# Squares and head sums moved to VectorE, and other banks for the indexer, in a two-layer decoder trunk

## The chip, the cores and the metric

The kernel runs on one core of a Trainium2 chip. The metric is the device time of one execution in microseconds, from runs of the whole program; the profile shows one further execution. The engines are TensorE (PE in the profile; its weight loads are PEld), VectorE (DVE), ScalarE (ACT), GpSimd (POOL) and SyncE (SP), which here only issues DMAs.

## The reference

A trunk of two layers over 512 tokens of width 1024, batch 1, float32. Layer 0 is a half-step SwiGLU, a mixer of Mamba-2 SSD heads and mLSTM heads, and a second half-step SwiGLU. Layer 1 is the same with sparse attention as its mixer. Before each of the six stages the tokens are normalized by their root mean square:

```
x = x + 0.5 * swiglu(rms_norm(x, ffn_norm[l, 0]), ...)
h = rms_norm(x, mix_norm[l]);  x = x + mixer(h)
x = x + 0.5 * swiglu(rms_norm(x, ffn_norm[l, 1]), ...)
rms_norm(x, g) = x * rsqrt(mean(x * x) + 1e-6) * g
```

The sparse attention (16 heads of 64, one shared key and value head) lets each query see only the 128 keys that an indexer scores highest. The indexer has 8 heads; its score is a weighted sum over them, with weights `wi` that depend on the query:

```
logits = einsum('bthd,bsd->btsh', qi, ki)
score  = einsum('btsh,bth->bts', relu(logits), wi) * idx_scale      # then causal mask
sel    = top_k(score, 128);  softmax attention over the selected keys
```

## The kernel before

All activations stay on the chip, transposed: `xT` holds the 1024 features in 8 chunks of 128 partitions, with the 512 tokens along the free dimension. Weights are streamed as float32 blocks through a ring of 4 raw buffers, and each is split into a high and a low part (ScalarE copies the high part, VectorE or an accumulating DMA makes the low one). A product is then three matmuls: high by high, high by low and low by high (`mm3`, lines 241 to 243).

**The order of the work.** Every operation is not issued at once but given to a `Plan` as a step, with an engine, an estimated duration, and the keys of what it reads and writes. At the end one list scheduler places the steps of the whole program: on each engine it takes the step that can start first by its estimates, and among those the one that is due first. TensorE's steps are kept in order within a stream; the attention stage has several streams ("filler", "index", "logits", "values"), and filler products have their due times pushed back (`plan.later`), so that they stand in gaps. Tiles with few buffers (`plan.BUFS`, PSUM banks among them) make a step wait for the users of the tile that had the buffer before. Each engine then runs its instructions in the order so written.

**The norm between stages.** When the stage before has finished a pair of chunks, `prep_later` (from line 634) makes, per chunk, the input times its gain in a high and a low part (L657 on ScalarE, L660 on VectorE) and its square (L669 on ScalarE). GpSimd adds the squares chunk by chunk to a running sum `ssq` (L356, called with `pool` true). The squares of the last two chunks are not added: they are appended to the list `ssqs`. `settle_later` (from line 615) is called twice by the next stage. The first call sums over the partitions on TensorE: for each member of `ssqs` and each of the four token blocks, a matmul with a column of ones (L327, tile `pssq`). VectorE then makes the mean (L624) and GpSimd the power of -1/2 (L626). The second call spreads the factors over the partitions with four transposes (L336, tile `prow`) and a copy on ScalarE (L630), which gives `rrow`. The products themselves start before `rrow` is known; they are scaled afterwards. In an FFN's first units (`unit`, from line 576) each of eight steps is a block of four products of 0.69 us by the planner, and the two calls stand behind the second and the fourth block (behind the third and the fifth where `late` is set, in the first FFN). The mixer of layer 0 calls `settle_later` at places of its own.

**The indexer in attention.** Seven jobs (`indexer`) project the tokens to the indexer's queries, keys and weights; a job is a product over 8 chunks into one PSUM bank, and `scaled` copies it out on ScalarE with the norm's factors (L1595). The first four jobs use banks `gm`, `po` and two of `lg`, and run before the factors are known; the last three use `gm`, `po` and `gm` again. Then, for each query block b = 1, 2, 3 with n = 256, 384 or 512 keys: rotary embedding on VectorE (L1507 to L1511), transposes (L1521), and four pairs of logits (L1665), one pair for two heads, into `lg` banks. ScalarE applies the relu into `rl` (L1672). GpSimd has made 8 diagonal matrices from the head weights (L1648); TensorE multiplies each `rl` by its diagonal and accumulates the 8 in one bank (`acc`, tag `pt`, L1656); ScalarE copies the sum into the mask's place (L1676); GpSimd sets the causal part (L1677). `topk` then runs 16 rounds on VectorE, each of a maximum of eight (L1883) and a replacement (L1884), and turns the scores into a mask (L1887). Meanwhile the filler stream makes the key and value projection and the attention's queries, and the softmax of the heads (L1784 logits, L1788 mask and maximum, L1800 exponentials, L1806, L1824 values) follows block by block, block 0 needing no top-k.

Of the kernel before, what the change touches and what calls it, by code (L numbers as in the profile page):

```python
# [16 lines left out]
P = 128  # L17
# [196 lines left out]
class Trunk:  # L214
# [361 lines left out]
    def unit(self, raws, stream, late, summed):  # L576
# [6 lines left out]
        for qs in ((0, 1), (2, 3)):  # L583
            for i in range(4):
# [6 lines left out]
                for s in range(2):  # L591
                    col = slice(s * P, (s + 1) * P)
                    for q in qs:
# [5 lines left out]
                        )  # L599
                if 2 * qs[0] + i in ((2, 4) if late else (1, 3)):  # L600
                    self.settle_later()
# [32 lines left out]
    def prep_later(self, which, k, last, squares=True, half=None):  # L634
# [18 lines left out]
        for j in (k, k + 1):  # L653
# [15 lines left out]
            self.s(n, lambda x=x, sq=sq: nc.scalar.activation(sq()[:, cols], x, AF.Square), self.xk(j, halves), sk)  # L669
            if last:  # L670
                self.ssqs, self.ssqk = self.ssqs + [(sq, halves[0] * NB // 2)], self.ssqk + sk
            elif j:
                part = [lambda x=x: x()[:, cols] for x in (ssq, sq)]
                self.vtt(n, part[0], *part, ALU.add, ["ssq"], ["ssq"] + sk, True)
        if last:
# [861 lines left out]
    def attention(self, nxt):  # L1537
# [23 lines left out]
        keep, kept = self.spot("keep", (4 * T,), 1)  # L1561
        diags, diagk = self.spot("diag", (2, 8, P), 1)
        two = [self.spot("pr", (2, 2 * T), 2) for _ in range(2)]
# [41 lines left out]
        scaled(jobs)  # L1605
        for b, g, tag in ((2, 1, "gm"), (3, 0, "po"), (3, 1, "gm")):
            jobs = [(b, g, self.bank(tag))]
            indexer(jobs, (0, 1, 2, 3, 6, 7, 4, 5))
            scaled(jobs)
# [17 lines left out]
        for b in range(NB):  # L1627
# [15 lines left out]

            acc, acck = self.bank("pt")
            diag = []
            for h in range(8):
                d, dk = lambda h=h, b=b: diags()[:, b % 2, h], (*diagk, b % 2, h)
                self.plan.add("gpsimd", 0.4, lambda d=d, t=t, h=h: nc.gpsimd.tensor_scalar(  # L1648
                    d(), self.ident, t()[:, WI + h : WI + h + 1], 0.0, op0=ALU.mult, op1=ALU.add), [xk], [dk])
                diag.append((d, dk))  # L1650
            rls = []

            def add(acc=acc, acck=acck, diag=diag, rls=rls, n=n):
                for h in range(len(rls) - 2, len(rls)):
                    (d, dk), (rl, rk) = diag[h], rls[h]
                    self.t(0.02 + 1.68e-3 * n, lambda h=h, d=d, rl=rl: nc.tensor.matmul(  # L1656
                        acc()[:, 0:n], d(), rl()[:, 0:n], start=h == 0, stop=h == 7), [dk, rk], [acck])

            for i in range(4):
                ps = [self.bank("lg") for _ in range(2)]  # L1660

                def pair(ps=ps, qiT=qiT, i=i, n=n):
                    for par in range(2):
                        hp = slice(par * 64, par * 64 + 64)
                        nc.tensor.matmul(ps[par][0]()[:, 0:n], qiT()[hp, i * P : (i + 1) * P], kiT()[hp, 0:n], start=True, stop=True)  # L1665

                self.t(0.1 + 1.68e-3 * n, pair, [qik] + [(*kik, s) for s in range(b + 1)], [ps[0][1], ps[1][1]])
                if i:
                    add()
                for par in range(2):  # L1670
                    rl, rk = self.spot("rl", (T,), 4)
                    self.s(n, lambda rl=rl, ps=ps, par=par, n=n: act(rl()[:, 0:n], ps[par][0]()[:, 0:n], AF.Relu, scale=IDX_SCALE),  # L1672
                           [ps[par][1]], [rk])
                    rls.append((rl, rk))
            add()
            self.s(n, lambda sc=sc, acc=acc, n=n: act(sc(), acc()[:, 0:n], AF.Copy), [acck], [sk])  # L1676
            self.p(64, lambda sc=sc, b=b, n=n: nc.gpsimd.affine_select(  # L1677
# [285 lines left out]
```

## Time and profile before

| | |
|---|---|
| runs, median of 3 | 2012.17 us (2010.16 to 2013.01) |
| profiled execution, own time | 2003.96 us |
| its span, first to last instruction | 2002.2 us |
| mean granted TensorE clock | 0.992 |
| TensorE busy, loads busy | 98%, 91% of the span |
| VectorE, ScalarE, GpSimd busy | 81%, 63%, 16% |

In a profile row of the page or of a grouping, the line of the kernel comes first (L327), then engine and operation, the tile written and the tiles read, the shapes, and the count; then busy time, the mean duration of one, and the idle time of the engine just before, with what ended it. A row of the timeline begins with start and duration in us; brackets at its end show idle time of that engine before it and what ended that. A row of a stretch shows its bounds and length, and then the busy time of PE, PEld, DVE, ACT and POOL with the instruction counts, the granted TensorE clock (1.00 is full speed), the DMA engines' busy share and GB/s. A matmul of two float32 operands that were not split counts as two instructions.

### The profile page before, as it was taken

The numbers are of one execution on the slowest core, as the hardware profiler recorded it, in microseconds if no ns is written. First come the engines' busy times: TensorE is split into PE (matmuls) and PEld (weight loads), VectorE is DVE, ScalarE is ACT, GpSimd is POOL, SyncE is SP. The second block draws the span as 40 slices with busy tenths as digits, with TensorE's granted clock in tenths as the row PEclk, the third lists the DMA queues.
The fourth block names the chain that finished last, engine by engine and source line by source line (L and its number), as shares of the span: only waits on it lengthen the run. The fifth ranks groups of instructions, "written<-read, shape, count | busy, mean of one in ns | idle before, by whom it ended". The sixth has DMA issues, their size and how long they took to land.

```text
span 2002.2 us, 36425 instructions
## 1 busy us (share of the span) xinstructions
PE 1956.5 (98%) x14674; PEld 1813.3 (91%) x14674; DVE 1627.8 (81%) x2373; ACT 1264.7 (63%) x1906; POOL 325.0 (16%) x401
## 2 busy tenths in 40 slices
PE   8999999999999999999999999999999999999998
PEld 6999999799888888999998999999866588999998
DVE  6888888887888558989788998878589647988886
ACT  6666656567777545766566566666747744757564
POOL 1000002222234110000012001001414521101010
PEclk9999999999999999999999999999899999999999
DMA  8566766467769342666654466565735202666564
GB/s 221 137 157 152 176 155 161 118 166 190 198 176 262 86 117 74 162 172 162 158 149 141 111 170 161 155 174 137 188 88 116 53 17 69 158 158 169 148 170 115
DMA packets 226609, 292.89 MB, mean 146 GB/s; under 512 B 15036, under 2 KB 196488, under 8 KB 225928
## 3 DMA queue, kind: packets, MB, share of 16 engines
q1 hardware_dynamic: 200728, 199.30, 32.2%
q0 software_dynamic: 25632, 91.24, 24.2%
q8 instruction: 115, 1.88, 0.4%
q14 instruction: 54, 0.44, 0.1%
q10 hardware_dynamic: 80, 0.02, 0.0%
HBM read 192.96 MB, written 6.33 MB: 100 GB/s over the span
## 4 chain that ended last, share of the span: by engine, by line
PE 76%; DVE 8%; DMA 8%; issue 5%; ACT 1%; POOL 1%; SPq 0%; POOLq 0%; ACTq 0%; DVEq 0%
PE pA L242 9%; PE pA L241 9%; PE pA L243 9%; PE pD L241 5%; PE pD L243 5%; PE pD L242 5%; DMA form<-raw 3%; PE hm L242 2%; PE hm L243 2%; PE hm L241 2%; PE pB L241 2%; PE pB L243 2%; PE pB L242 2%; DMA raw<-in_hy_w_in 2%; DVE raw L356 2%
## 5 line engine op out<-in xcount | busy, mean ns | idle before, releaser
L363 DVE TENSOR_TENSOR form<-raw,form 128x1024 fp32r<-128x1024 f32 (+2 forms) x382 | 454.9, 1195 | 101.5 <-ACT form L361 100.0
L361 ACT ACTIVATE form<-raw 128x1024 fp32r<-128x1024 f32 (+2 forms) x382 | 392.1, 1030 | 206.0 <-DVE raw L356 142.4
L392 POOL DMA_DIRECT2D form<-raw x172 | 150.9, 879 | 1344.3 <-ACT form L391 1298.3
L356 DVE TENSOR_TENSOR raw<-raw 128x1024 f32<-128x1024 f32 (+2 forms) x281 | 333.2, 1190 | 22.8 <-DMA raw<-in_ffn_w_down 9.0
L241 PE MATMUL pA<-xf,form 128*128 128x256 f32 x1152 | 321.2, 279 | 0.0
L243 PE MATMUL pA<-xf,form 128*128 128x256 f32 x1152 | 320.7, 278 | 0.0
L242 PE MATMUL pA<-xf,form 128*128 128x256 f32 x1152 | 320.7, 278 | 0.0
L391 ACT ACTIVATE form<-raw 128x1024 fp32r<-128x1024 f32 (+1 forms) x172 | 178.2, 1037 | 161.6 <-PE pD L243 74.4
L241 PEld LDWEIGHTS pA<-xf,form 128*128 128x128 f32 x1152 | 217.2, 188 | 0.3
L243 PEld LDWEIGHTS pA<-xf,form 128*128 128x128 f32 x1152 | 217.3, 189 | 0.0
L242 PEld LDWEIGHTS pA<-xf,form 128*128 128x128 f32 x1152 | 217.0, 188 | 0.2
L242 PE MATMUL pA<-hid,form 128*128 128x256 f32 x704 | 198.2, 282 | 3.3 <-DVE hid L363 3.3
L241 PE MATMUL pA<-hid,form 128*128 128x256 f32 x704 | 198.0, 281 | 0.6 <-ACT hid L361 0.5
L243 PE MATMUL pA<-hid,form 128*128 128x256 f32 x704 | 197.2, 280 | 0.0
L393 ACT ACTIVATE form<-raw 128x1024 fp32r<-128x1024 f32 (+1 forms) x172 | 176.5, 1027 | 0.0
L241 PE MATMUL pD<-xf,form 128*128 128x256 f32 x576 | 160.3, 278 | 0.0
L243 PE MATMUL pD<-xf,form 128*128 128x256 f32 x576 | 160.2, 278 | 0.0
L242 PE MATMUL pD<-xf,form 128*128 128x256 f32 x576 | 160.2, 278 | 0.0
L356 DVE TENSOR_TENSOR ft<-ft 128x256 f32<-128x256 f32 (+2 forms) x296 | 151.3, 543 | 3.6
L242 PEld LDWEIGHTS pA<-hid,form 128*128 128x128 f32 x704 | 132.4, 188 | 5.2 <-DVE hid L363 5.1
L241 PEld LDWEIGHTS pA<-hid,form 128*128 128x128 f32 x704 | 132.6, 188 | 1.4 <-ACT hid L361 0.7
L508 ACT ACTIVATE ft<-pA 128x512 f32<-128x512 f32 x120 | 71.5, 595 | 97.7 <-PE pA L243 90.0
(441 smaller groups left out, 5427.6 us busy)
## 6 DMA issues: line engine op xcount, KB each, us to landing
form<-raw POOLq DMA_DIRECT2D x156, 512.0 KB, 5.9
raw<-in_ffn_w_gate SPq DMA_DIRECT2D x88, 512.0 KB, 3.9
raw<-in_ffn_w_up SPq DMA_DIRECT2D x88, 512.0 KB, 4.1
raw<-in_ffn_w_down SPq DMA_DIRECT2D x64, 512.0 KB, 4.0
raw<-in_hy_w_in SPq DMA_DIRECT2D x44, 512.0 KB, 4.7
raw<-in_ffn_w_down SPq DMA_DIRECT2D x32, 384.0 KB, 3.1
raw<-in_hy_w_out SPq DMA_DIRECT2D x16, 512.0 KB, 4.2
form<-raw POOLq DMA_DIRECT2D x16, 384.0 KB, 4.2
```

Source lines behind the costliest of these rows:

```text
L241: mm(out, l[0], r[0], start=start, stop=False)
L242: mm(out, l[0], r[1], start=False, stop=False)
L243: mm(out, l[1], r[0], start=False, stop=stop)
L356: (self.p if pool else self.v)(n, lambda: e.tensor_tensor(out(), x(), y(), op=op), reads, writes)
L361: self.s(n, lambda: nc.scalar.activation(hi(), src(), AF.Copy), srck, hik)
L363: n, lambda: nc.vector.tensor_tensor(lo(), src(), hi().bitcast(F32), op=ALU.subtract), srck + hik, lok
L391: self.s(n, lambda: nc.scalar.activation(f()[:, 1], raw, AF.Copy, scale=-1.0), rawk, lok)
L392: self.plan.add("gpsimd", 0.85, lambda: nc.gpsimd.dma_start(f()[:, 1], raw, accum_op=ALU.add), rawk + lok, lok, 5.5)
L393: self.s(n, lambda: nc.scalar.activation(f()[:, 0], raw, AF.Copy), rawk, hik)
L508: self.s(T, lambda: nc.scalar.activation(to(), ps()[:, :, 0:H], AF.Copy), [(*psk, 0), (*psk, 1)], tok)
```

## The change

Four edits.

In `unit`, the two calls of `settle_later` stand behind the third and the fourth block, where they stood behind the second and the fourth (the `late` case stays).

In `prep_later`, the squares of the last two chunks are added to the running sum too, by VectorE (`vtt` with `pool` false), so that `ssqs` has one member. This holds for all five norms between stages.

In `attention`, the last three jobs of the indexer use the banks `pt`, `pt` and the third `lg`.

In `attention`, the diagonals, their products, the bank `acc` and the copy out of it are gone. For each head VectorE multiplies `rl` by the head's weight, a column of the projection, and adds it to the scores in place (`scalar_tensor_tensor`; a `tensor_scalar` for the first head).

```
-                if 2 * qs[0] + i in ((2, 4) if late else (1, 3)):
+                if 2 * qs[0] + i in ((2, 4) if late else (2, 3)):
                     self.settle_later()
...
-            if last:
-                self.ssqs, self.ssqk = self.ssqs + [(sq, halves[0] * NB // 2)], self.ssqk + sk
-            elif j:
+            if j:
                 part = [lambda x=x: x()[:, cols] for x in (ssq, sq)]
-                self.vtt(n, part[0], *part, ALU.add, ["ssq"], ["ssq"] + sk, True)
+                self.vtt(n, part[0], *part, ALU.add, ["ssq"], ["ssq"] + sk, not last)
...
-        diags, diagk = self.spot("diag", (2, 8, P), 1)
...
-        for b, g, tag in ((2, 1, "gm"), (3, 0, "po"), (3, 1, "gm")):
+        for b, g, tag in ((2, 1, "pt"), (3, 0, "pt"), (3, 1, "lg")):
             jobs = [(b, g, self.bank(tag))]
             indexer(jobs, (0, 1, 2, 3, 6, 7, 4, 5))
             scaled(jobs)
...
-            acc, acck = self.bank("pt")
-            diag = []
-            for h in range(8):
-                d, dk = lambda h=h, b=b: diags()[:, b % 2, h], (*diagk, b % 2, h)
-                self.plan.add("gpsimd", 0.4, lambda d=d, t=t, h=h: nc.gpsimd.tensor_scalar(
-                    d(), self.ident, t()[:, WI + h : WI + h + 1], 0.0, op0=ALU.mult, op1=ALU.add), [xk], [dk])
-                diag.append((d, dk))
-            rls = []
-
-            def add(acc=acc, acck=acck, diag=diag, rls=rls, n=n):
-                for h in range(len(rls) - 2, len(rls)):
-                    (d, dk), (rl, rk) = diag[h], rls[h]
-                    self.t(0.02 + 1.68e-3 * n, lambda h=h, d=d, rl=rl: nc.tensor.matmul(
-                        acc()[:, 0:n], d(), rl()[:, 0:n], start=h == 0, stop=h == 7), [dk, rk], [acck])
...
-                if i:
-                    add()
                 for par in range(2):
                     rl, rk = self.spot("rl", (T,), 4)
+                    h = 2 * i + par
+                    wi = lambda t=t, h=h: t()[:, WI + h : WI + h + 1]
                     self.s(n, lambda rl=rl, ps=ps, par=par, n=n: act(rl()[:, 0:n], ps[par][0]()[:, 0:n], AF.Relu, scale=IDX_SCALE),
                            [ps[par][1]], [rk])
-                    rls.append((rl, rk))
-            add()
-            self.s(n, lambda sc=sc, acc=acc, n=n: act(sc(), acc()[:, 0:n], AF.Copy), [acck], [sk])
+                    if h:
+                        self.v(n + 60, lambda rl=rl, sc=sc, wi=wi, n=n: v.scalar_tensor_tensor(
+                            sc(), rl()[:, 0:n], wi(), sc(), op0=ALU.mult, op1=ALU.add), [rk, xk, sk], [sk])
+                    else:
+                        self.v(n, lambda rl=rl, sc=sc, wi=wi, n=n: v.tensor_scalar(
+                            sc(), rl()[:, 0:n], wi(), 0.0, op0=ALU.mult, op1=ALU.add), [rk, xk], [sk])
```

## The prediction

> **What bounds the kernel now.** I read the page's busy shares and its chain of waits first, then busy time by stretches, then the timeline at the places that the change touches.
>
> ```profile
> span 2002.2 us, 36425 instructions
> PE 1956.5 (98%) x14674; PEld 1813.3 (91%) x14674; DVE 1627.8 (81%) x2373; ACT 1264.7 (63%) x1906; POOL 325.0 (16%) x401
> PE 76%; DVE 8%; DMA 8%; issue 5%; ACT 1%; POOL 1%; SPq 0%; POOLq 0%; ACTq 0%; DVEq 0%
> ...
> 1447.00:1454.00 7.00, 7.00 (x40) 5.26 (x37) 0.00 (x0) 4.37 (x10) 2.23 (x5) 1.00 1.01 187
> 1454.00:1577.00 123.00, 117.09 (x541) 72.62 (x539) 104.90 (x320) 79.72 (x182) 45.06 (x68) 0.99 0.38 84
> ...
> 1538.00:1577.00 39.00, 33.09 (x176) 17.97 (x174) 29.15 (x94) 34.21 (x87) 22.81 (x36) 0.96 0.20 41
> ```
>
> TensorE is the bound: 98% busy, and 76% of the chain that ended last is its work. So a TensorE instruction that goes away is worth its own time, unless TensorE then waits for something else. The last three rows (columns: stretch, length, then busy us of PE, PE loads, DVE, ACT, POOL, the granted clock, DMA) are the attention stage, from the indexer's first block to the first logits of the last block. TensorE idles 123.00 - 117.09 = 5.9 us there, all of it after 1538 (39.00 - 33.09), when the products that fill its gaps have run out. VectorE, at 104.90 of 123 us, is the nearest second bound.
>
> **1. The sums of squares.** Five times, at each norm between stages, 24 one-column matmuls (12 in two passes) sum the squares over features: 8 for the running sum and 8 for each of the two last squares that were left apart. The change adds those two on VectorE, so 8 of 24 stay.
>
> ```profile
> 359.12 2.73 PE L327 MATMUL pssq<-raw,ssq 128*128 128x1 f32 x24
> ...
> 1429.89 2.73 PE L327 MATMUL pssq<-raw,ssq 128*128 128x1 f32 x24
> ...
> 1661.16 3.55 PE L327 MATMUL pssq<-raw,ssq 128*128 128x1 f32 x24 [0.88 <-POOL ssq L356]
> ```
>
> 2.73 us for 24 is 0.114 us each; 16 fewer are 1.82 us, and five places give **9.1 us**. TensorE is busy on both sides in all five, so I take it whole.
>
> At the norm before the last FFN TensorE also waited 0.88 us for the running sum. The change puts the sums one block of products later in a unit, which covers this wait: **0.9 us**, and what is late next is the second step, the row of factors. Both steps now have one block between them instead of two. The two rows below bound a block: its first product starts at 1669.84 and the transposes of the factors follow at 1672.62, 2.8 us. From the sums' end to the factors I count from the two rows after: VectorE's step 0.1 us behind the last matmul (1085.14 + 2.74), then GpSimd's power until 1088.15 + 1.47 = 1089.62, together 1.8 us. It fits with 1 us to spare; if VectorE has one 1.2 us split ahead of its step, the stall is 0.2 us. I take nothing.
>
> ```profile
> 1669.84 0.43 PE L241 MATMUL pu<-xgn,form 128*128 128x512 f32 x1
> ...
> 1672.62 0.60 PE L336 MATMUL prow<-raw 128*128 128x128 f32 x4
> ...
> 1085.14 2.74 PE L327 MATMUL pssq<-raw,ssq 128*128 128x1 f32 x24
> ...
> 1087.91 0.16 DVE L624 TENSOR_SCALAR raw<-pssq 128x4 f32<-128x4 f32 x1
> 1088.15 1.47 POOL L626 TENSOR_TENSOR raw<-raw 128x4 f32<-128x4 f32 x1 [5.58 <-DVE raw L624]
> ...
> 352.54 0.41 PE L242 MATMUL hc<-xgn,form 128*24 128x512 f32 x1 [1.30 <-DVE xgn L660]
> ...
> 1081.49 0.50 PE L242 MATMUL pg<-xgn,form 128*128 128x512 f32 x1 [1.01 <-DVE xgn L660]
> ```
>
> The price is on VectorE: two adds of 128x512 at 0.69 us (the L718 row below) in each of five places, 6.9 us in all. Behind them on VectorE stand conversions of the normalized input (L660) and splits of weights. Where VectorE is idle they cost nothing; in the two rows above TensorE already waits 1.30 and 1.01 us for L660. Bounds: 0, and all 6.9 us on the path. The adds need the last squares, and so come after most of the conversions that TensorE waits for; I charge **1.0 us**.
>
> **2. The clock.** Four stretches below hold or follow these sums.
>
> ```profile
> 360.00:370.00 10.00, 10.00 (x48) 8.37 (x48) 2.75 (x5) 1.08 (x2) 1.04 (x1) 0.83 0.34 99
> 750.00:760.00 10.00, 10.00 (x60) 8.69 (x59) 6.05 (x21) 0.88 (x2) 1.53 (x3) 1.00 0.18 54
> 1085.00:1095.00 10.00, 10.00 (x60) 8.70 (x59) 5.30 (x8) 1.74 (x3) 1.47 (x1) 1.00 0.51 160
> 1430.00:1440.00 10.00, 8.96 (x55) 8.52 (x54) 3.38 (x10) 3.83 (x11) 5.45 (x9) 0.72 1.03 261
> 1440.00:1450.00 10.00, 10.00 (x63) 8.33 (x62) 2.14 (x4) 7.90 (x15) 6.87 (x12) 0.94 0.42 105
> 1660.00:1670.00 10.00, 9.12 (x40) 7.76 (x39) 2.91 (x5) 2.50 (x5) 2.12 (x2) 0.66 0.12 42
> ```
>
> After three of the five bursts the granted clock falls (0.83; 0.72 with 0.94; 0.66): 1.7, 2.8 + 0.6 = 3.4 and 3.4 us of full-speed time lost, 8.5 us in all. After the other two it stays at 1.00, so the same 2.73 us burst does it only sometimes, as if activity were judged over fixed stretches not much longer than the burst. A burst of 8, 0.9 us, should be too short. Bounds: 0 (other causes keep them) and 8.5 us. I take the two dear ones, **6.8 us**, and leave 1.7 us for a new stretch where TensorE will wait more, in attention.
>
> The Trainium skill ("TensorE: Matmul & The Clock Gate", section "Why this matters for your kernels") says that the clock falls back after an idle gap of about 3 us. Here TensorE was busy through the bursts at 359 and idle for under 1 us around 1430 and 1661, so the trace does not follow that rule as written; by it the burst would not matter and this term would be 0.
>
> **3. The weighted sum over heads.** It removes 48 matmuls (24 in two passes), 24 diagonals on GpSimd and 3 copies on ScalarE.
>
> ```profile
> L1648 POOL TENSOR_SCALAR diag<-raw,pr 128x128 f32<-128x128 f32 x24 | 13.9, 634 | 2.1 <-ACT pr L1595 2.1
> ...
> L1656 PE MATMUL pt<-rl,diag 128*128 128x512 f32 x16 | 7.7, 605 | 0.0
> ...
> L1656 PE MATMUL pt<-rl,diag 128*128 128x384 f32 x16 | 6.0, 506 | 0.0
> ...
> L1656 PE MATMUL pt<-rl,diag 128*128 128x256 f32 x16 | 4.3, 398 | 0.0
> ...
> 1481.10 3.60 PE L1656 MATMUL pt<-rl,diag 128*128 128x512 f32 x8
> 1484.13 0.79 PE L241 MATMUL gm<-form,xgn 128*128 128x512 f32 x1
> ```
>
> Busy time is 7.7 + 6.0 + 4.3 = 18.0 us with overlapping tails. By starts, the eight of 512 columns took 1484.13 - 1481.10 = 3.03, 0.379 each; scaled by columns 16 x 0.379 x (512 + 384 + 256) / 512 = 13.6 us. I take 15 us of TensorE. GpSimd's 13.9 us cover nothing: it is 16% busy.
>
> What it adds is VectorE work, priced from these rows (128x512 scalar_tensor_tensor; 128x256 of two tensors; a 384-wide form at its least 0.547; tensor_scalar of 256, 384 and 512):
>
> ```profile
> L718 DVE SCALAR_TENSOR_TENSOR raw<-ft,raw x72: 677/691/1758, 116.6 to 1994.4; 128x512 f32<-128x512 f32 x72
> L356 DVE TENSOR_TENSOR raw<-lg,raw x16: 411/424/425, 1630.4 to 1660.3; 128x256 f32<-128x256 f32 x16
> L1788 DVE CUSTOM_DVE_ANT_0 pw<-lg,keep x32: 547/610/692, 1548.7 to 1605.6; 128x384 f32<-128x384 f32 x16, 128x512 f32<-128x512 f32 x16
> L1887 DVE TENSOR_SCALAR keep<-keep x3: 329/355/424, 1472.2 to 1554.1; 128x256 f32<-128x256 f32 x1, 128x384 f32<-128x384 f32 x1, 128x512 f32<-128x512 f32 x1
> 1454.28 0.43 DVE L1883 MAX8 keep<-keep 128x8 f32<-128x256 f32 x1 [12.11 <-POOL keep L1677]
> ```
>
> Block 1: 7 x 0.42 + 0.36 = 3.3 us, covered by the 12.11 us in which VectorE waits for that block's scores. Block 2: 7 x 0.55 + 0.33 = 4.2; block 3: 7 x 0.69 + 0.42 = 5.2. These 9.4 us fall among the top-k rounds, so VectorE has 104.9 + 9.4 = 114.3 us to do before the last logits begin. At 95% full that is 120 us instead of 123, so 3 us earlier; block 1's scores lose a sum behind each pair of heads, and top-k starts some 2.5 us earlier. So the last logits come 5.5 us earlier, not 15: the rest of TensorE's saving becomes waiting, into which I let 2.5 us of the output products move. This term: **8 us**. Bounds: -9.4 (VectorE's work all on the path, TensorE's saving all waiting) and 15.
>
> **4. The banks.** The indexer's three later jobs get banks that nothing holds.
>
> ```profile
> 1434.49 0.44 PE L243 MATMUL gm<-iw,xgn 128*128 128x292 f32 x1
> 1435.72 0.48 PE L1521 MATMUL pq<-raw,ri 128*128 128x128 f32 x1 [0.79 <-ACT ri L1533]
> ```
>
> The products of the first such job ran on to 1434.49, before TensorE idled 0.79 us for ScalarE; that is a step of the written order, and the wait may go or stay. Between 0 and 0.8 I take 0.
>
> **The sum.** 9.1 + 0.9 - 1.0 + 6.8 + 8 + 0 = 23.8 us. The profiled execution took 2003.96 (span 2002.2 and 1.8 around it): 2003.96 - 23.8 = 1980.2. The runs' median, 2012.17, is 0.41% above that execution, so 1980.2 x 1.0041 = **1988 us**. One planner places all instructions of the program, so a changed step reorders others; 3 us either way are in the range for that.
>
> **The rivals.**
> *VectorE becomes the bound of attention.* For it: 104.90 of 123 us. Against it, block 3's top-k ends 30 us before its logits start, so it has that to give:
>
> ```profile
> 1545.49 0.68 DVE L1884 MATCH_REPLACE8 keep<-keep 128x512 f32<-128x512 f32 x1
> ...
> 1576.22 1.13 PE L1784 MATMUL lg<-keys,rq 64*128 64x512 f32 x4
> ```
>
> Term 3 is then 0, and the time 1988 + 8 = 1996.
> *The clock does not care* (the skill's rule, or stretches that come from elsewhere): term 2 is 0, 1988 + 6.8 = 1995. For it: two of five bursts without effect. Against it: the three falls follow the bursts.
> *The adds eat the sums:* VectorE's 6.9 us land ahead of the conversions that TensorE waits for. Then term 1 loses another 5.9, 1994. For it: the 1.30 and 1.01 us waits; against: the squares come last.
> *Slower.* In attention the in-order VectorE, with its 9.4 us more, sits ahead of the softmax of blocks 1 and 2; TensorE runs out of fillers 15 us sooner, and its waits between 1520 and 1577 keep the clock at half. Price: +9.4 for VectorE, and six lost stretches of 1.7 us for the clock, 10.2; less 15.8 from terms 1 and 2: 2012 + 4 = 2016. It decides if VectorE is full until after block 3's logits could have begun. Against it: those 30 us.
> *More than forecast:* all 8.5 us of clock and 15 of term 3: 1988 - 1.7 - 7 = 1979.
>
> **How the numbers follow.** Forecast 0.45; VectorE bound 0.18; clock 0.14; adds 0.10; more 0.05; slower mechanism 0.08, of which 0.03 end within 0.2% (4 us, about what a measurement can tell from no change). Faster 0.92, same 0.03, slower 0.05. The range runs from 1976, the largest gain and the planner's 3 us, to 2003, where two of the smaller-gain rivals hold at once (1996 + 6.8).
>
> **What would show it.** Each burst of sums: 8 matmuls, under 1.0 us, and a clock of 1.00 in the 10 us after. At 1661 no wait for the running sum. No diagonal rows; 24 new VectorE rows of 0.42 to 0.7 us; top-k of block 1 starting before 1450 on the old scale. More TensorE idle between 1520 and 1577 than 5.9 us, up to 13. I am wrong if the clock falls after an 8-burst, if the block-3 logits start less than 3 us sooner relative to the stage's start, or if TensorE waits for L660 or for the factors more than 3 us in all.

## The result, and the profile after

The change runs in 2000.25 us (median of 17 runs, 1993.64 to 2014.76) beside 2013.01 us for the kernel before (17 runs, 1998.89 to 2017.64) on the same chip: ratio 0.9945, interval 0.9929 to 0.9962. It is faster, by 0.55% or 11 us by this ratio (the two medians alone are 12.8 us apart). The forecast was a gain of 24 us and a time of 1988 us; the time lies in the range, but the gain is less than half of the forecast.

The page of the change, its span, busy times and chain of waits:

```profile
span 1997.0 us, 36148 instructions
PE 1942.3 (97%) x14546; PEld 1797.1 (90%) x14546; DVE 1643.4 (82%) x2407; ACT 1264.1 (63%) x1903; POOL 311.1 (16%) x377
PE 73%; DVE 10%; DMA 8%; issue 5%; ACT 2%; POOL 1%; SPq 0%; ACTq 0%; POOLq 0%; DVEq 0%
```

From one profiled execution to the other TensorE lost 14.2 us of busy time (1956.5 to 1942.3), but the span lost only 5.2: TensorE waits more, and three points of its share of the chain went to VectorE and ScalarE.

The timeline at the sums of squares (start, duration, instruction, idle time before it), first, fourth and last of the five places, and the transposes of the factors; the row at 1649.47 is the first of the block of products that now stands ahead of the sums at the last place:

```profile
361.05 1.02 PE L327 MATMUL pssq<-raw,ssq 128*128 128x1 f32 x8 [1.10 <-DVE ssq L356]
...
366.15 0.82 PE L336 MATMUL prow<-raw 128*128 128x128 f32 x4
...
1430.63 0.95 PE L327 MATMUL pssq<-raw,ssq 128*128 128x1 f32 x8
...
1649.47 0.39 PE L241 MATMUL pu<-xgn,form 128*128 128x512 f32 x1
...
1659.79 1.49 PE L327 MATMUL pssq<-raw,ssq 128*128 128x1 f32 x8 [2.88 <-DVE ssq L356]
...
1666.40 0.93 PE L336 MATMUL prow<-raw 128*128 128x128 f32 x4
```

A burst is 8 matmuls and takes about 1 us, 1.49 at the last place, where the clock has fallen (0.66 in the stretch from 1660 below). TensorE now waits 2.88 us at the last place, where it waited 0.88, and for VectorE's add (L356) in the place of GpSimd's; at the first place it waits 1.10 us for the same add, where it had no wait. From the sums to the factors it is 6.6 us instead of 11.5 (1661.16 to 1672.62 before), but this is not all gain: 2.8 us of the difference are the block of products that now runs at 1649.47, ahead of the sums, and about 2 us are the shorter burst.

The stretches behind three of the sums, and two in attention (stretch, length, busy us of PE, PE loads, DVE, ACT, POOL, granted clock, DMA share, GB/s):

```profile
360.00:370.00 10.00, 8.95 (x38) 7.43 (x39) 4.75 (x10) 0.85 (x2) 1.05 (x1) 0.83 0.58 187
...
1430.00:1440.00 10.00, 10.00 (x79) 10.00 (x79) 5.24 (x13) 5.26 (x13) 1.03 (x1) 1.00 1.03 254
1440.00:1450.00 10.00, 10.00 (x53) 6.98 (x51) 2.82 (x6) 7.59 (x14) 2.66 (x3) 1.00 0.99 211
1660.00:1670.00 10.00, 10.00 (x37) 8.23 (x37) 3.22 (x7) 0.70 (x2) 1.02 (x1) 0.66 0.01 2
...
1530.00:1540.00 10.00, 6.85 (x32) 3.88 (x31) 9.72 (x26) 9.47 (x22) 5.52 (x10) 0.83 0.43 99
1600.00:1610.00 10.00, 8.47 (x36) 4.37 (x36) 2.89 (x9) 6.81 (x17) 5.28 (x8) 0.83 0.00 0
```

The clock's fall behind the fourth place is gone (0.72 and 0.94 before). Those at 360 and 1660 are not, and in attention there are two falls, at 1530 and 1600, where the profile before had one, at 1571.

The groups of VectorE's new rows (duration least/median/most in ns, first and last start in us, forms):

```profile
L1657 DVE SCALAR_TENSOR_TENSOR keep<-rl,pr,keep x21: 475/619/752, 1446.1 to 1493.2; 128x256 f32<-128x256 f32 x7, 128x384 f32<-128x384 f32 x7, 128x512 f32<-128x512 f32 x7
L1660 DVE TENSOR_SCALAR keep<-rl,pr x3: 399/409/478, 1443.9 to 1469.4; 128x256 f32<-128x256 f32 x1, 128x384 f32<-128x384 f32 x1, 128x512 f32<-128x512 f32 x1
```

Each is about 0.06 us dearer than priced: 12.9 + 1.3 = 14.2 us for the 24, where the prediction had 3.3 + 9.4 = 12.7.

**How the runs are read below.** Each timed execution has its span and its mean granted TensorE clock c, which is given to 0.001, 2 us of this span. I split the span into span x c, what it would be at full clock if TensorE set the pace throughout, and span x (1 - c), what the clock took, and average each over the executions of a kernel. Over 92 executions of the kernel before, the span grows by 1.04 us for each us taken, so the split holds for it. It tells apart two things that the ratio adds up. A +- is one standard error. Kernels of one batch ran on one chip beside the kernel before.

| kernel | ratio, 95% interval | span at full clock, us | taken by the clock, us |
|---|---|---|---|
| before (92 executions, batches 1 to 5) | 1 | 1988.8 +- 0.3 | 17.8 +- 0.4 |
| the change, first timing (17) | 0.9945 [0.9929, 0.9962] | 1980.6 +- 0.4 | 19.1 +- 0.9 |
| batch 1: squares_alone | 0.9929 [0.9904, 0.9953] | 1979.9 +- 0.8 | 12.8 +- 1.0 |
| heads_alone | 0.9985 [0.996, 1.001] | 1984.5 +- 0.7 | 20.4 +- 1.3 |
| last_squares_left_out | 0.9939 [0.9917, 0.996] | 1977.8 +- 0.9 | 17.0 +- 0.9 |
| block3_on_tensor | 0.9905 [0.9873, 0.9938] | 1978.4 +- 0.9 | 9.9 +- 1.0 |
| batch 2: change_topk_10_of_16 | 0.9932 [0.9906, 0.9959] | 1976.7 +- 1.3 | 15.6 +- 1.9 |
| before_topk_10_of_16 | 0.998 [0.9959, 1.0] | 1985.6 +- 1.0 | 16.9 +- 1.3 |
| all_blocks_on_tensor | 0.9927 [0.9904, 0.9951] | 1978.9 +- 1.3 | 12.3 +- 1.1 |
| block3_on_gpsimd | 0.9933 [0.9911, 0.9955] | 1977.0 +- 1.4 | 14.9 +- 0.9 |
| batch 3: change_block2_topk_10 | 0.9928 [0.9903, 0.9953] | 1977.0 +- 1.5 | 14.5 +- 1.4 |
| tensor_block2_topk_10 | 0.9925 [0.9904, 0.9946] | 1979.1 +- 0.9 | 11.6 +- 0.6 |
| change_block2_first | 0.9988 [0.9972, 1.0004] | 1983.3 +- 0.9 | 19.9 +- 0.9 |
| block3_on_tensor_block2_first | 0.9926 [0.9902, 0.9949] | 1979.1 +- 0.8 | 12.6 +- 1.9 |
| batch 4: change_again | 0.9955 [0.9937, 0.9972] | 1980.8 +- 0.9 | 15.3 +- 1.2 |
| change_topk_9_13 | 0.9917 [0.9887, 0.9947] | 1976.3 +- 1.3 | 13.9 +- 2.3 |
| tensor_topk_9_13 | 0.9935 [0.9917, 0.9953] | 1978.1 +- 1.1 | 13.6 +- 1.4 |
| change_rope_on_gpsimd | 0.9926 [0.9906, 0.9946] | 1975.1 +- 0.8 | 15.3 +- 1.5 |
| batch 5: tensor_rope_on_gpsimd | 0.9946 [0.9923, 0.9968] | 1980.8 +- 0.7 | 14.2 +- 1.3 |
| block3_on_tensor_rope | 0.9915 [0.9889, 0.9941] | 1979.2 +- 1.3 | 10.0 +- 1.5 |

### The profile page after: what moved, and what is told of

Same layout as the page of the kernel before. It is cut to its first block, busy times and chain, and to the rows that moved or that the text cites. A ratio compares the mean times of both kernels' runs of the same rounds, so it can differ in the third digit from the quotient of the medians.

```text
span 1997.0 us, 36148 instructions
## 1 busy us (share of the span) xinstructions
PE 1942.3 (97%) x14546; PEld 1797.1 (90%) x14546; DVE 1643.4 (82%) x2407; ACT 1264.1 (63%) x1903; POOL 311.1 (16%) x377
## 4 chain that ended last, share of the span: by engine, by line
PE 73%; DVE 10%; DMA 8%; issue 5%; ACT 2%; POOL 1%; SPq 0%; ACTq 0%; POOLq 0%; DVEq 0%
PE pA L242 8%; PE pA L241 8%; PE pA L243 8%; PE pD L241 4%; PE pD L243 4%; PE pD L242 4%; DMA form<-raw 3%; PE hm L241 3%; PE hm L242 3%; PE hm L243 3%; DMA raw<-in_ffn_w_down 3%; PE pB L241 2%; PE pB L243 2%; PE pB L242 2%; DVE form L363 2%
## 5 line engine op out<-in xcount | busy, mean ns | idle before, releaser
L356 DVE TENSOR_TENSOR raw<-raw 128x1024 f32<-128x1024 f32 (+2 forms) x281 | 332.5, 1188 | 23.9 <-DMA raw<-in_ffn_w_down 15.6
L356 DVE TENSOR_TENSOR ft<-ft 128x256 f32<-128x256 f32 (+2 forms) x296 | 151.3, 543 | 3.5
L242 PEld LDWEIGHTS pA<-hid,form 128*128 128x128 f32 x704 | 133.0, 189 | 6.8 <-DVE hid L363 6.7
L243 PEld LDWEIGHTS pA<-hid,form 128*128 128x128 f32 x704 | 133.2, 189 | 3.9 <-DVE form L363 3.9
L241 PEld LDWEIGHTS pA<-hid,form 128*128 128x128 f32 x704 | 133.3, 189 | 3.3 <-DVE ft L356 1.6
```

What stands on the lines that cost most here:

```text
L241: mm(out, l[0], r[0], start=start, stop=False)
L242: mm(out, l[0], r[1], start=False, stop=False)
L243: mm(out, l[1], r[0], start=False, stop=stop)
L356: (self.p if pool else self.v)(n, lambda: e.tensor_tensor(out(), x(), y(), op=op), reads, writes)
```

## The experiments

**Batch 1: the norms or attention?** Theory N: the norms lost the gain. Rival A: attention ate it.

*squares_alone* is the kernel before with the first two edits:

```
-                if 2 * qs[0] + i in ((2, 4) if late else (1, 3)):
+                if 2 * qs[0] + i in ((2, 4) if late else (2, 3)):
...
-            if last:
-                self.ssqs, self.ssqk = self.ssqs + [(sq, halves[0] * NB // 2)], self.ssqk + sk
-            elif j:
+            if j:
...
-                self.vtt(n, part[0], *part, ALU.add, ["ssq"], ["ssq"] + sk, True)
+                self.vtt(n, part[0], *part, ALU.add, ["ssq"], ["ssq"] + sk, not last)
```

> The kernel before with the edit in prep_later and the one in unit alone; attention's indexer and its banks as before. Theory N (the gain went missing in the norms: the adds on VectorE make the running sum late, so that TensorE waits at the norms before mixer 0 and before the last FFN, 1.1 and 2.9 us in the trace after, and its clock still falls there): 2 to 5 us faster than before. Rival A (the gain went missing in attention, the norms gave what was forecast): 13 to 17 us faster. The forecast had 15.8 us for these two edits.

Measured 0.9929, 14 us: 8.9 +- 0.9 us at full clock and 5.0 +- 1.1 of the clock. The norms gave nearly all that they were forecast to give (15.8). Theory N falls.

*heads_alone* is the kernel before with the fourth edit only (the diagonals, their products and the copy out; VectorE's `scalar_tensor_tensor` in).

> The kernel before with the weighted sum over heads on VectorE alone; squares, the calls of settle_later and the banks as before. Theory N: 6 to 9 us faster, as forecast (8). Rival A: 0, between 3 us faster and 3 us slower, because VectorE is full between 1500 and 1580 us and block 3's top-k ends 36 us later than before.

Measured 0.9985, 3 us. The weighted sum on VectorE gains 4.3 +- 0.8 us at full clock and costs 2.6 +- 1.4 of clock.

*last_squares_left_out*:

```
-            if j:
+            if j and not last:
                 part = [lambda x=x: x()[:, cols] for x in (ssq, sq)]
-                self.vtt(n, part[0], *part, ALU.add, ["ssq"], ["ssq"] + sk, not last)
+                self.vtt(n, part[0], *part, ALU.add, ["ssq"], ["ssq"] + sk, True)
```

> The changed kernel, but the squares of the last two chunks are neither added nor summed (so the norms are of six chunks of eight): 8 one-column matmuls as in the change, and no add on VectorE. Theory N: 5 to 9 us faster than the changed kernel, so 16 to 20 us faster than before, with no wait for the running sum at 1660 us and fewer falls of the clock. Rival A: within 2 us of the changed kernel, 9 to 13 us faster than before.

Measured 0.9939, which the ratio can't tell from the change's 0.9945; at full clock it is 2.8 +- 1.0 us shorter. So the adds cost nothing by the ratio and about 3 us at full clock: the rival in which they eat the sums (6.9 us) falls.

*block3_on_tensor*, the change with one block's sum put back as it was before:

```
+            onpe, rls, diag = b in (3,), [], []
...
-                    if h:
+                    if onpe:
+                        rls.append((rl, rk))
+                    elif h:
```

> The changed kernel, but for query block 3 the weighted sum is made as before, by diagonals on TensorE; blocks 1 and 2 on VectorE. It takes 5.7 us from VectorE (7 of 0.752 us and one of 0.478) and gives TensorE about 6.5 us back. Theory N (attention did what was forecast, VectorE has slack to give): slower than the changed kernel by 1 to 4 us. Rival A (VectorE bounds attention): faster than the changed kernel by 1 to 5 us.

Measured 0.9905, the best ratio of the study, with the least taken by the clock, 9.9 us. By its median it gains on the change by undoing a third of the fourth edit; the two intervals overlap.

**Batch 2: is it VectorE's amount of work?** Theory V: the amount of VectorE's work bounds attention. Rival W: the chain of the softmax in its written order does.

*change_topk_10_of_16* and *before_topk_10_of_16*:

```
-        for r in range(TOPK // 8):
+        for r in range(TOPK // 8 if n < T else 10):
```

> The changed kernel with 10 of 16 top-k rounds for query block 3 (so its queries attend to 80 keys, not 128): 6 x 1.52 = 9.1 us less work on VectorE, nothing else changed. Theory V (VectorE's amount of work sets the length of attention in the changed kernel): 5 to 9 us faster than the changed kernel, 16 to 20 us faster than before. Rival W (what holds attention is the chain of softmax steps and the order they are written in; VectorE is full but others set the end): within 2 us of the changed kernel.

> The kernel before with the same cut of block 3's top-k to 10 of 16 rounds: the control. Theory V: VectorE had 30 us to give there, so 0 to 2 us faster than before. Rival W: the same 0 to 2 us. A gain of 5 us or more would mean that VectorE's work was a bound before the change too, against the forecast's reading of the trace.

Measured 0.9932 and 0.998. By ratios the cut is worth 2.6 us to the change and 4 us to the kernel before: no support for V. At full clock it is 4.0 +- 1.4 and 3.2 +- 1.0 us, which are not told apart either.

*all_blocks_on_tensor* is the change without its fourth edit (`onpe` is `b in (1, 2, 3)`).

> The changed kernel with the weighted sum of all three query blocks by diagonals on TensorE, so the edits to the squares and the banks without the one to the heads. Theory V: slower than block3_on_tensor by 2 to 6 us, since TensorE gets back blocks 1 and 2, 8 to 9 us of work, and VectorE loses only 4.75 us that mattered: 13 to 17 us faster than before. Rival W: like block3_on_tensor within 2 us. Against squares_alone it shows the banks: the forecast has 0 for them.

Measured 0.9927 against 0.9929 of squares_alone: the banks of the third edit are worth nothing that can be seen. And it is not slower than the change: with edits 1 to 3 in place, edit 4 gains nothing.

*block3_on_gpsimd*: block 3's sum on GpSimd, as a `tensor_scalar` and a `tensor_tensor` for each head in the place of VectorE's one instruction.

> The changed kernel, but block 3's weighted sum is made on GpSimd: 8 products of 0.69 us (as L1806) and 7 adds of 1.5 us (as L356), 16 us on an engine that is 16% busy; VectorE loses 5.7 us, TensorE gets nothing back. Theory V: as fast as block3_on_tensor or up to 5 us faster, 19 to 24 us faster than before, if block 3's top-k can start some 10 us later. Rival W: within 2 us of the changed kernel.

Measured 0.9933: no better than with the block on TensorE, and at full clock 3.7 us below the change. The batch left V undecided.

**Batch 3: VectorE ahead of one mask, or the order?** Theory M: VectorE is late with block 2's mask. Rival O: the gain is lost elsewhere. In *change_block2_topk_10* and *tensor_block2_topk_10* the top-k of block 2 is cut in the change and in all_blocks_on_tensor:

```
+        for r in range(TOPK // 8 if n != 3 * P else 10):
```

> The change with the top-k of block 2 cut from 16 rounds of max and match-replace to 10 (it leaves out the last six rounds of block 2, so block 2 keeps fewer positions; every other step is the change). VectorE has 6 x 1.2 = 7 us less to do ahead of block 2's mask (row of the change: 1542.22 0.35 DVE L1872). Theory M (edit 4 frees TensorE 15 us sooner, but block 2's mask is still written by VectorE only about 6 us sooner than before, so the softmax of blocks 2 and 3 waits for VectorE and the gain is given back): the 7 us come back nearly whole, ratio to before 0.991, and against the control with the weighted sum on TensorE and the same cut the change is ahead by 5 us or more. Rival O (the gain is lost elsewhere on TensorE: order of products, clock): 0.9935, and no more than 1 us ahead of the control.

> The control: edits 1, 2 and 3, the weighted sum of every block with diagonals on TensorE, and the same cut of block 2's top-k to 10 rounds of 16 (the last six rounds of block 2 left out). On its own side TensorE is still doing the weighted sums while VectorE runs block 2's top-k. Theory M: little comes of it, at most 2 us, ratio 0.992 to 0.9925. Rival O: the same gain as in the change, 0.9915.

Measured 0.9928 and 0.9925. The control stood still, as M has it (1978.9 to 1979.1 at full clock), the change fell from 1980.7 to 1977.0; but the change did not get ahead of the control by 5 us as M wanted.

*change_block2_first* and *block3_on_tensor_block2_first*:

```
-            plan.later = 60.0 * (b > 1)
+            plan.later = {1: 0.0, 2: 20.0, 3: 60.0}[b]
```

> The change, with the due times of top-k pushed back by 20 us for block 2 and 60 us for block 3 instead of 60 for both: VectorE runs four rounds of block 3's top-k (4 x 1.5 = 6 us) after block 2's mask instead of before it. No work is left out. Theory M: block 2's mask at about 1536 instead of 1542.2, and 3 to 6 us less in all: ratio 0.992 to 0.993. Rival O: 0.9945 as the change, as the same work is done in another order.

> Block 3's weighted sum on TensorE, those of blocks 1 and 2 on VectorE, and top-k pushed back by 20 us for block 2 and 60 us for block 3. Where block 3's sum is on TensorE block 2's mask already comes at 1533.6, with one round of block 3 among its last. Theory M: at most 1.5 us better than the same kernel with 60 us for both, ratio 0.990. Rival O: 0.9905. What it is for besides: whether the version with block 3 on TensorE is again faster than the change (0.9945).

Measured 0.9988 and 0.9926. In the first, block 2's mask came at 1533.38, as meant, and the kernel lost most of what the change had gained. M falls: block 2's mask is not what decides. The timeline of VectorE points at another step (the mask of block 2; the first row of block 3's softmax mask):

```profile
1533.38 0.36 DVE L1872 TENSOR_SCALAR keep<-keep 128x384 f32<-128x384 f32 x1
...
1584.66 0.69 DVE L1773 CUSTOM_DVE_ANT_0 pw<-lg,keep 128x512 f32<-128x512 f32 x1
```

In the change these stand at 1542.22 and 1583.09: what went behind block 2's mask came ahead of block 3's, and that one came no earlier. The 1.6 us by which it came later are not the whole loss of some 9 us by the ratio (2.6 +- 1.0 at full clock).

**Batch 4: the amount again, with the right control.** Theory A: VectorE's extra work delays block 3's mask, TensorE waits, and the waits cost clock. Rivals: O as above, and C, that the change's clock loss belonged to the chip of the first timing.

*change_again* is the change itself.

> The change itself, timed beside the kernels of this batch. Theory A (VectorE's extra work delays block 3's mask, TensorE waits in attention, and these waits also cost clock): ratio 0.9945, with 17 to 20 us of the span lost to the clock, against 17 to 18 for before and 12 for edits 1 to 3. Rival C (the larger clock loss belonged to the chip of the first timing): lost to the clock no more than 14 us, ratio 0.9925.

Measured 0.9955, with 15.3 +- 1.2 us taken by the clock. The expectation of neither theory is met, but a part of C holds: the 19.1 of the first timing was high, on a chip where the kernel before took 2013 us too, beside 2007 to 2010 in the batches. Against 12.3 +- 1.1 with the sums on TensorE it is 3.0 +- 1.6 more. The span at full clock repeats to 0.2 us.

*change_topk_9_13* and *tensor_topk_9_13*:

```
+        for r in range({2 * P: 16, 3 * P: 9, 4 * P: 13}[n]):
```

> The change with the top-k of block 2 cut from 16 rounds to 9 and of block 3 to 13 (the last seven and three rounds left out: 7 x 1.2 + 3 x 1.5 = 13 us of VectorE's work). Theory A: TensorE no longer waits for VectorE in attention, so the weighted sum's gain shows: ratio 0.989 to 0.991, full-clock span 1974 or less, and at least 4 us ahead of the control tensor_topk_9_13. Rival O (what eats the gain is not VectorE): 0.9935 and level with the control.

> The control: edits 1 to 3, the weighted sum of all blocks by diagonals on TensorE, and the same cut of the top-k (9 rounds in block 2, 13 in block 3; the rest left out). TensorE's own 15 us for the sums still stand. Theory A: 0.9915 to 0.9925, full-clock span 1977 to 1979. Rival O: the same as change_topk_9_13 within 1 us.

Measured 0.9917 and 0.9935: 4.4 us less at full clock in the change and 0.8 in the control. The direction is A's; the distance is not (1976.3 against the 1974 asked for).

*change_rope_on_gpsimd*, and its control *tensor_rope_on_gpsimd* in batch 5, move work and leave none out:

```
-        self.v(n * 64, lambda: v.tensor_tensor(p1(), x(), cos(), op=ALU.mult), [xk, *reads, ("raw", "sum")], [k1])
+        e = self.nc.gpsimd if pool else v
+        (self.p if pool else self.v)(n * 64, lambda: e.tensor_tensor(p1(), x(), cos(), op=ALU.mult), [xk, *reads, ("raw", "sum")], [k1])
...
-            self.rope(x3, xk, 8, cos, sin, [tk(2), tk(3)], rq, rqk)
+            self.rope(x3, xk, 8, cos, sin, [tk(2), tk(3)], rq, rqk, True)
```

> The change, with one of the two full products of the queries' rotation (x times cosine, 128x512, eight times, 0.68 us each on VectorE) on GpSimd; nothing is left out. GpSimd took 1.67 us for a 128x512 product of two tensors, and the rotation's next step waits for it, about 1 us more in each of the eight chains. VectorE has 5.4 us less to do between the first logits and block 3's mask. Theory A: block 3's first mask row 4 to 5 us sooner in its distance to the first logits (103 us in the change), ratio 0.992 to 0.993. Rival O: 0.9945 to 0.996, no gain or the later chains cost.

> The control of change_rope_on_gpsimd: edits 1 to 3, the weighted sum of all blocks by diagonals on TensorE, and the cosine product of the queries' rotation on GpSimd; nothing is left out. Theory A (VectorE's amount of work bounds attention only when the weighted sum is on it too): no gain over edits 1 to 3, ratio 0.992 to 0.9935, full-clock span 1978 to 1980. Rival G (GpSimd is simply the better place for this product): 0.990 and a full-clock span of 1975 or less.

Measured 0.9926 and 0.9946: the same edit takes 5.6 +- 0.9 us off the change at full clock, and adds 1.9 +- 1.5 to the control. GpSimd is not the better place in itself (rival G falls); it helps where VectorE has too much. The product took GpSimd 1.33 us on average in change_rope_on_gpsimd (L1507, eight of them), less than the 1.67 of the expectation. The first logits and block 3's mask in change_rope_on_gpsimd:

```profile
1473.55 0.49 PE L1770 MATMUL lg<-keys,rq 64*128 64x128 f32 x4
...
1574.35 0.69 DVE L1774 CUSTOM_DVE_ANT_0 pw<-lg,keep 128x512 f32<-128x512 f32 x1
```

They are 100.8 us apart, 103.3 in the change: 2.5 us, and not the 4 to 5 expected, so not all of the 5.6 is seen at this mask.

*block3_on_tensor_rope* joins the two remedies (the rotation's product on GpSimd for blocks 2 and 3).

> Block 3's weighted sum on TensorE, those of blocks 1 and 2 on VectorE, and the cosine product of the queries' rotation of blocks 2 and 3 on GpSimd (four of the eight); nothing is left out. Theory A: block 3's sum (about 6 us) is already off VectorE there and little more comes of 2.7 us: full-clock span 1977 to 1979, ratio 0.990 to 0.992. Rival G: 1975 or less, 0.989.

Measured 0.9915, with 1979.2 +- 1.3 at full clock: as A expected, the two do not add up. The three kernels with block 3 on TensorE, medians 1988.96, 1991.52 and 1990.49 us, are by their ratios 19, 15 and 17 us below the kernel before, where the change is 11 and 9 in its two timings. The interval of block3_on_tensor (to 0.9938) lies below the change's 0.9945 but overlaps with its interval, so it is the better version by its median, and by how much stays open.

## Why the prediction was right, and where it failed

**Term 1, the sums (9.0 us net): right in its total, in part by luck.** Edits 1 and 2 alone took 8.9 +- 0.9 us off the span at full clock. The bursts gave what was counted: the five rows together went from 14.5 to 5.4 us. The wait at the last place did not go: 0.88 us became 2.88, behind VectorE's add, and 1.10 us came at the first place. Together the waits are 3.1 us longer, where the prediction had 0.9 of gain and 1.0 of cost; that is about what the adds cost at full clock in last_squares_left_out (2.8 +- 1.0). So the rows account for some 6 of the 8.9 us; where the other 3 come from no run shows.

**Term 2, the clock (6.8 us): right in kind, and somewhat large.** Edits 1 and 2 alone gave 5.0 +- 1.1 us. That the shorter burst did it is read from counts: no run changes the burst's length and nothing else. "A burst of 8 should be too short" is refuted: the clock falls at 360 and 1660 above. But it falls less often. Of the 20 profiles (18 of experiments), 3 have bursts of 24 and 17 bursts of 8. Behind the first place the clock fell in 3 of 3, and in 4 of 17; behind the second in 2 of 3, and never; behind the fourth in 2 of 3, and never; at the last place it always fell, for 5.7 us on average, and for 4.4. A fall is to half speed, so half of its length is lost; by these counts the shorter burst is worth 4.8 us, and a fall just ahead of the third place, in 8 of the 17 and in none of the 3, takes 0.8 back. The rival by the Trainium skill's rule ("TensorE: Matmul & The Clock Gate", section "Why this matters for your kernels": the clock falls back after an idle gap of about 3 us) would have made this 0; the 5.0 +- 1.1 us are against it here, though the fall at the last place of the change does follow a wait near that length (2.88 us).

**Term 4, the banks (0): right** (0.9927 against 0.9929).

**Term 3, the weighted sum (8 us): this step failed.** On top of edits 1 to 3 it costs 1.9 +- 1.6 us at full clock and 3.0 +- 1.6 of clock (the change in batch 4 against all_blocks_on_tensor in batch 2). Each of the two is less than two standard errors from nothing; what is clear is that the gain of 8 us did not come. In the kernel before, alone, it gains 4.3 and loses 2.6. The bounds, -9.4 to 15, held it. Four places in the trace show why: the last products of the FFN ahead, the first logits of block 0, the row in which VectorE has block 3's mask ready (a `TENSOR_SCALAR` of 128x512 on `keep`), and the first row of block 3's softmax that uses it. The timeline of the kernel before:

```profile
1411.86 0.28 PE L241 MATMUL pA<-hid,form 128*128 128x256 f32 x1
...
1494.84 0.49 PE L1784 MATMUL lg<-keys,rq 64*128 64x128 f32 x4
...
1554.10 0.42 DVE L1887 TENSOR_SCALAR keep<-keep 128x512 f32<-128x512 f32 x1
...
1578.07 0.69 DVE L1788 CUSTOM_DVE_ANT_0 pw<-lg,keep 128x512 f32<-128x512 f32 x1
```

The timeline of the change, with the start of block 3's logits besides:

```profile
1417.94 0.28 PE L241 MATMUL pA<-hid,form 128*128 128x256 f32 x1
...
1479.80 0.49 PE L1769 MATMUL lg<-keys,rq 64*128 64x128 f32 x4
...
1556.65 1.13 PE L1769 MATMUL lg<-keys,rq 64*128 64x512 f32 x4 [0.93 <-DVE raw L1789]
...
1582.52 0.43 DVE L1872 TENSOR_SCALAR keep<-keep 128x512 f32<-128x512 f32 x1
1583.09 0.69 DVE L1773 CUSTOM_DVE_ANT_0 pw<-lg,keep 128x512 f32<-128x512 f32 x1
```

The timeline of all_blocks_on_tensor, the control, with the start of block 3's logits and the last sums of squares:

```profile
1419.41 0.42 PE L241 MATMUL pA<-hid,form 128*128 128x256 f32 x1
...
1490.01 0.49 PE L1792 MATMUL lg<-keys,rq 64*128 64x128 f32 x4
...
1564.37 1.13 PE L1792 MATMUL lg<-keys,rq 64*128 64x512 f32 x4
...
1570.14 0.41 DVE L1895 TENSOR_SCALAR keep<-keep 128x512 f32<-128x512 f32 x1
...
1574.44 0.69 DVE L1796 CUSTOM_DVE_ANT_0 pw<-lg,keep 128x512 f32<-128x512 f32 x1 [1.40 <-PE po L1832]
...
1660.11 1.02 PE L327 MATMUL pssq<-raw,ssq 128*128 128x1 f32 x8 [2.91 <-DVE ssq L356]
```

Counted from the FFN's last products, the first logits come after 83.0 us before, 70.6 in the control and 61.9 in the change: edit 4 alone brought TensorE there 8.7 us sooner. But block 3's mask is ready after 142.2, 150.7 and 164.6 us, and first used after 166.2, 155.0 and 165.2. So it lay ready for 24.0 us before, for 4.3 in the control and for 0.6 in the change. In the control, without edit 4, most of VectorE's lead is gone already (in squares_alone it is 21.0 us, so the planner's order alone can move it); edit 4, whose new rows take 14.2 us, made the mask ready 13.9 us later and its first use 10.1 us later. Both engines meet in block 3's softmax, and the sums of squares behind attention start after 240.7 us in the control (1660.11) and 241.9 in the change (1659.79).

VectorE's load up to that mask is read from stretches (columns as above). From the FFN's last products to the mask in the change, a part of it in which TensorE waits, and attention from the first logits to the last output product:

```profile
1417.90:1583.10 165.20, 154.81 (x851) 107.63 (x850) 138.33 (x390) 114.76 (x242) 61.64 (x84) 0.99 0.52 121
...
1524.70:1556.70 32.00, 23.64 (x116) 12.20 (x114) 31.26 (x97) 24.79 (x55) 12.22 (x20) 0.95 0.48 115
...
1479.80:1656.60 176.80, 164.11 (x933) 111.58 (x933) 131.62 (x368) 101.28 (x225) 61.77 (x88) 0.98 0.26 61
```

The first and the last of these in the control:

```profile
1419.40:1574.40 155.00, 151.90 (x777) 104.08 (x777) 120.76 (x355) 107.07 (x229) 64.84 (x98) 0.98 0.48 109
...
1490.00:1656.90 166.90, 163.80 (x975) 116.25 (x975) 113.93 (x321) 101.90 (x227) 61.05 (x88) 1.00 0.28 64
```

VectorE has 17.6 us more to do ahead of block 3's mask than in the control, 14.2 of them the new rows. In the change, from 1524.7 to 1556.7, it is busy for 31.26 of 32 us, and TensorE for 23.64.

The sentence that failed is the argument against the first rival: "block 3's top-k ends 30 us before its logits start, so it has that to give". Before, the top-k's last row was at 1545.49 and the logits started at 1576.22. In the change the logits start at 1556.65 and the mask is made at 1582.52, 26 us behind them; in the control, without edit 4, the logits start at 1564.37 and the mask is made at 1570.14. The 30 us were not VectorE's to give: it was busy for 20.4 of them (1546.2 to 1576.2 in the kernel before) and idle for 9.6, hardly more than the 9.4 us that it was to get. And they were the distance between two steps, which move when TensorE comes sooner. How the rows stand fits with this reading: the softmax is ready sooner, and takes VectorE's turns ahead of top-k rounds; no run holds the order fixed to show it. So the sign that I had named for this term, block 3's logits less than 3 us sooner, did not show (they come 138.7 us behind the FFN instead of 164.4) and was the wrong one; the mask was the step to name. Rival one, with the term at 0 and 1996 us, was nearest, and the slower rival's mechanism (waits in attention that cost clock) took part: its clock at 3.0 us of the 10.2 priced.

Four of TensorE's waits ahead of block 3's logits, on the timeline of the change (in brackets the wait, and for whom; the last is for the rotated queries):

```profile
1528.47 0.33 PE L1519 MATMUL pt<-raw,pn 128*128 128x128 f32 x1 [1.07 <-POOL pn L1791]
...
1533.46 2.45 PE L1809 MATMUL po<-pT,keep 128*64 128x512 f32 x4 [1.88 <-ACT pT L1525]
...
1538.46 0.39 PE L242 MATMUL gm<-oh,form 128*128 128x256 f32 x1 [1.27 <-DVE oh L1819]
...
1555.07 0.66 PE L1519 MATMUL pq<-raw,q 128*128 128x128 f32 x4 [2.61 <-DVE q L1509]
```

From the first logits to the last output product TensorE is busy for about the same time in the change and in the control (164.11 and 163.80 us), but idles for 12.7 us against 3.1, and the clock is 0.98 against 1.00. In 8 of the 9 profiles with the whole weighted sum on VectorE the clock fell between 1521 and 1540, where the first three of these waits stand. From first logits to last output product it took 3.6 us on average in those nine, 1.2 in the seven with it all on TensorE, and nothing in the three with block 3 on TensorE.

That VectorE's amount of work is the cause rests on the pairs: with 5 to 13 us of it gone, by a cut top-k or by GpSimd, the change's span at full clock fell by 3.7 to 5.6 us, and that of the version with the sums on TensorE moved by -0.8 to +1.9. The pair with the rotation (5.6 +- 0.9 off, 1.9 +- 1.5 on) is clear of noise by itself; in each of the other two the difference within the pair, some 4 us, is less than two standard errors. Three things stay open. The gain does not grow with the work taken away: 13 us gave 4.4, and 5.4 us gave 5.6. The cut top-k of block 3 gained 3.2 us in the kernel before too, where by this account VectorE had room. And with VectorE relieved the change is 2 to 6 us ahead of its control at full clock and not 8; no run tells whether the planner's order or another engine holds the rest.

## What to carry to other kernels

The distance between two steps in a trace is slack only for an engine that is idle in it, and only as long as neither step moves. Before a gap is given away, sum what the engine that takes the new work has to do up to the step where both engines meet, in the order in which it will do it once the other engine is early; here that work came to 10 us too much, and by the medians a third of the edit left on TensorE was better than all of it moved. And when a time moves less than it should, split it into the span at full clock and what the clock took: here a gain of 9 us, one of 5 by the clock and a loss of some 5 had added up to a number that fitted no theory.

## What the runs showed of the hardware

The granted clock falls without any long pause. In the kernel before, TensorE was busy for all ten us behind 360, and the clock was 0.83 on average. In the change, in the ten us behind 1530, TensorE's longest wait was 1.88 us and it was busy for 6.85, and the clock was 0.83 on average. In the record of the clock each fall is to half speed and lasts a multiple of 3.41 us, but for the one that the end of the program cuts off. Where the falls stand differs from one profile to the next of the same kernel: the change had them at 1534 and 1605 in one, and at 1535 and 1559 in the other. So the clock alone spreads the times: in the 92 executions of the kernel before it took 10 to 28 us, with a standard deviation of 3.9 us, beside 2.9 us of the span at full clock.

An add in place on VectorE with a factor per partition (128x256, 384 and 512 columns, float32) took 0.48, 0.62 and 0.75 us; the same instruction on line L718, from which it was priced, had taken 0.69 at 512.
